# The down product of a feed-forward group, cut into pieces that run between the next group's gate and up products

## The chip, the cores and the metric

The kernel runs on one core of one Trainium2 chip. The metric is the device time of one execution in microseconds (us). Engines are named as in the profile: PE (matrix products; PEld is its weight load), DVE (vector engine), ACT (scalar engine, which reads PSUM and applies functions), POOL (GpSimd), SP (which issues most DMAs). PE's results lie in PSUM tiles, from which DVE and ACT read them; the kernel counts PSUM in banks of 128 x 512 fp32 values and hands out eight in the part that changes.

## What is computed

Two model blocks one after the other on 512 tokens of width 1024 (528 tokens in the second one, with 16 meta tokens ahead). The second block has two layers, and each ends in the feed-forward part that the change touches:

```python
def conv_ffn(h, w_up, w_gate, conv_w, conv_b, w_down):
    u = h @ w_up
    g = h @ w_gate
    g = lax.conv_general_dilated(g, conv_w[:, None, :], window_strides=(1,),
                                 padding=[(CONV_WIDTH - 1, 0)], ...) + conv_b
    return (jax.nn.silu(g) * u) @ w_down

h = h + conv_ffn(rmsnorm(h, norm_ffn[l]), ...)       # l = 0, 1
return rmsnorm(h, norm_final)[:, N_META:N_META + S]
```

The inner width is 2816 = 22 feature blocks of 128. Everything is fp32; the kernel splits each operand into a rounded high part and a low remainder and adds three products (high x high, low x high, high x low) for each matrix product.

## The kernel before, in words

Activations stand transposed: features on the 128 partitions, tokens along the row. `X` (eight blocks of 128 features) is the residual stream. `ffn(l, out)` (L1052) runs the feed-forward part twice: for l = 0 with 528 columns, for l = 1 with 512 and with the final norm at its end.

- `seven` (L1109) prepares the normed input as the right operands of seven half-size products.
- `paired` (L1158) makes one gate or up product for the two feature blocks i and i + 11 at once. It loads two weight tiles, adds and splits them (DVE at L1170 and L157, ACT at L156), and then runs seven products of 12 matmuls each. In the program's order these are 1, 5, 6, 2, 7, 4, 3. Products 1, 6, 7, 4 add up in one bank (`pa`, tag "a", two buffers), 5 and 3 in `pc`, 2 in `pb` (one tile of two banks, tag "mm"). After product 7 ACT copies `pa` to `f` (L1204), and product 4 must wait for that copy, because it adds to `pa`. DVE adds `pc` to `f` (L1205) before product 3. Afterwards L1208 adds both banks to the result `e`, and L1095 or L1100 read `pa`.
- One round i of the loop (L1086) is a gate `paired`, the convolution, silu (ACT, L1074) and a multiplication on POOL (L1075), an up `paired`, and the products of both, split into `aH`, `aL` (`done`, L1078).
- Rounds stand in groups (0,3), (3,6), (6,9), (9,11) (L1083). After a group, `added` (L685) multiplies its 6 (or 4) feature blocks with the down weights: for each of eight output blocks o one weight tile (`weights`, L138: DMA on SP's queue, ACT rounds, DVE subtracts) and 36 matmuls (18 of double width for 512 columns), and then DVE adds the PSUM tile to `X` (L695). I call these eight products a burst. The last group of l = 1 goes through `final` (L1211), which also makes the final norm; its eight products per half of the columns take PSUM tiles of tags "mm" and "a" in turn.
- `Banks` (L36) hands out PSUM: tag "mm" turns over the mm pools, here two of two banks each; "t" and "a" have two single banks each.

The order of instructions on each engine is set by a scheduler from the program's order, dependencies and buffers; each engine then runs its list strictly in that order, and waits for others by semaphores. The code that makes it:

Of the kernel before, what the change touches and what calls it, by code (L numbers as in the profile page):

```python
# [9 lines left out]
F32 = mybir.dt.float32  # L10
F32R = mybir.dt.float32r
AF = mybir.ActivationFunctionType
OP = mybir.AluOpType
# [5 lines left out]
S = 512  # L19
# [11 lines left out]
def two(x):  # L31

    return x.rearrange("p (a b) -> p a b", a=2)


class Banks:  # L36
# [7 lines left out]
    def tile(self, *args, tag, bufs, **opts):  # L44
        if tag == "mm":
            tag, bufs, self.n = f"mm{self.n % self.mm}", 1, self.n + 1
        return self.pools[tag].tile(*args, tag=tag, bufs=bufs, **opts)


class Norm:  # L50
# [42 lines left out]
class Net:  # L93
# [617 lines left out]
    W = 1360  # L711
# [340 lines left out]
    def ffn(self, l, out=None):  # L1052

        nc, d = self.nc, self.d
        X, n, u = (self.X, T2, 0) if l == 0 else (self.X[:, :, TAIL:], S, NM - TAIL)
        lead, w = u or 2, n + u
        m = w // 2
        self.tb, self.mm = 2, 2
        with ExitStack() as c:
            pp = Banks(self.tc, c, "ffn", "mm1 t a mm0")  # L1060
            fp = c.enter_context(self.tc.tile_pool(name="ffn", bufs=1))
            new = lambda name, cols, bufs, dt=F32: fp.tile([128, cols], dt, name=name, tag=name, bufs=bufs)
            cw = fp.tile([128, 22, 4], F32, name="cw")
            nc.gpsimd.dma_start(cw, d[f"conv_{l}"])
            ops, rs = self.seven(pp, fp, X, self.gain[:, 6 + l])
            act = [], []

            def activated(i, g):

                z = new("z", n, 4)  # L1070
                nc.scalar.activation(z, g[:, lead:], AF.Identity, scale=cw[:, i, 2:3], bias=cw[:, i, 3:4])  # L1071
                for k in range(2):
                    nc.vector.scalar_tensor_tensor(z, g[:, lead - 2 + k:lead - 2 + k + n], cw[:, i, k:k + 1], z, op0=OP.mult, op1=OP.add)  # L1073
                nc.scalar.activation(z, z, AF.Silu)  # L1074
                nc.gpsimd.tensor_tensor(z, z, rs[:, u:], op=OP.mult)  # L1075
                return z

            def done(z):  # L1078
                act[0].append(new("aH", n, 7, F32R))
                act[1].append(new("aL", n, 7, F32R))  # L1080
                self.split(act[0][-1], act[1][-1], z)

            for a, b in ((0, 3), (3, 6), (6, 9), (9, 11)):  # L1083
                act[0].clear()
                act[1].clear()
                for i in range(a, b):  # L1086
                    g = [new("g", lead + n, 3) for _ in range(2)]
                    if u == 0:
                        for t in g:
                            nc.vector.memset(t[:, :2], 0.0)  # L1090
                    e = g[0][:, lead - u:]
                    f, t = self.paired(pp, fp, d[f"gate_{l}"], i, ops, e, m)
                    nc.vector.tensor_tensor(e, e, rs, op=OP.mult)
                    nc.vector.scalar_tensor_tensor(g[1][:, lead - u + m:], f, -1.0, rs[:, m:], op0=OP.mult, op1=OP.mult)
                    nc.vector.scalar_tensor_tensor(g[1][:, lead - u:lead - u + m], t, -1.0, rs[:, :m], op0=OP.mult, op1=OP.mult)  # L1095
                    z = [activated(i + 11 * j, g[j]) for j in range(2)]
                    e = new("u", w, 2)
                    f, t = self.paired(pp, fp, d[f"up_{l}"], i, ops, e, m)
                    nc.vector.scalar_tensor_tensor(z[1][:, m - u:], f, -1.0, z[1][:, m - u:], op0=OP.mult, op1=OP.mult)
                    nc.vector.scalar_tensor_tensor(z[1][:, :m - u], t[:, u:], -1.0, z[1][:, :m - u], op0=OP.mult, op1=OP.mult)  # L1100
                    nc.vector.tensor_tensor(z[0], z[0], e[:, u:], op=OP.mult)
                    for t in z:
                        done(t)
                if out is None or b < 11:
                    self.added(pp, d[f"down_{l}"], act, 2 * a, 2 * b, X[:, :, u:])
                else:
                    self.final(pp, fp, d[f"down_{l}"], act, 2 * a, 2 * b, out)

    def seven(self, pp, fp, x, g):  # L1109

# [44 lines left out]
            nc.scalar.activation(rs[:, a:b], out, AF.Copy)  # L1155
        return right, rs

    def paired(self, pp, fp, src, i, right, e, m):  # L1158


        nc, wp = self.nc, self.wp
# [21 lines left out]
        h, l = half(new("wy", 1))  # L1183
# [6 lines left out]
        def product(ps, j, start=False):  # L1190
            (wh, wl), (bh, bl) = left[j], right[j]
            for k in range(4):
                for v, (p, q) in enumerate(((wh, bh), (wh, bl), (wl, bh))):
                    nc.tensor.matmul(ps, p[:, k], q[k], start=start and k == 0 and v == 0, stop=k == 3 and v == 2, skip_group_check=not start)  # L1194

        f = fp.tile([128, T2 // 2], F32, name="f", tag="f", bufs=2)[:, :m]
# [6 lines left out]
        product(pa, 7)  # L1203
        nc.scalar.activation(f, pa, AF.Copy)  # L1204
        nc.vector.tensor_tensor(f, f, pc, op=OP.add)  # L1205
        product(pa, 4)
        product(pc, 3)
        nc.vector.tensor_tensor(two(e), two(e), pt[:, :, :m], op=OP.add)  # L1208
        return f, pa

    def final(self, pp, fp, src, act, a, b, out):  # L1211


        nc, x, m = self.nc, self.X[:, :, NM:], S // 2
        W = [[(0, b - a, self.weights(src[o, :, a:b], o >= 4))] for o in range(8)]
        rows = [fp.tile([128, T2], F32, name="o", tag="op", bufs=12) for _ in range(8)]
        for i in range(2):
            c = slice(m * i, m * i + m)
            sums, y = self.sums(pp, m, 8, 1), [t[:, c] for t in rows]
            for o in range(8):  # L1220
                _, _, ps = self.bank(pp, 0, m, ("mm", "a")[o % 2], 2)
                for k, e, w in W[o]:
                    self.dense([([(ps, c)], w)], (act[0][k:e], act[1][k:e]), k == 0, e == b - a)
                nc.vector.tensor_tensor(x[:, o, c], x[:, o, c], ps, op=OP.add)
                sums(x[:, o, c])
                nc.scalar.activation(y[o], x[:, o, c], AF.Copy, scale=self.gain[:, 8, o:o + 1])
            rs = self.row_tile("rs", m)
            (ps, _, _), = self.rstd(pp, sums, 1.0 / D)
            nc.scalar.activation(rs, ps, AF.Copy)
            for k in range(8):  # L1230
                if k in (5, 7):
                    nc.gpsimd.tensor_tensor(y[k], y[k], rs, op=OP.mult)
                else:
                    nc.vector.tensor_tensor(y[k], y[k], ps, op=OP.mult)  # L1234
                (nc.sync if k % 2 else nc.scalar).dma_start(out[:, k, c], y[k])
# [118 lines left out]
```

## Time and profile before

| what | value |
|---|---|
| three runs | 2217.07, 2216.91, 2213.74 us; median 2216.91 us |
| profiled execution | 2216.71 us, of which the span of its instructions is 2215.0 us |
| PE busy | 2052.8 us, 93% of the span |
| DVE busy | 1488.5 us, 67% |
| ACT busy | 986.6 us, 45% |
| granted PE clock over the span | 0.98 of full speed |

Busy time is the time in which an instruction of the engine runs. For PE it hides something: a matmul is recorded longer than the distance to the next one, so a short pause between two matmuls is partly covered by the record of the first. The rows further down are windows (busy time by engine in a stretch), waits (for whom an engine stood idle), timelines and groups of instructions. Times in windows and timelines count from the start of the span.

### The profile page before, as it was taken

Reading aid. Unit: us, or ns where it says so; the run is one execution under the profiler, and the core shown is the slowest. Engines: PE = TensorE matmul, PEld = TensorE weight load, DVE = VectorE, ACT = ScalarE, POOL = GpSimd, SP = SyncE. Lnnn points to the kernel's source line nnn. Section 1 sums busy time; section 2 is a strip of 40 time slices with the busy share of each in tenths; the row PEclk is TensorE's granted clock in tenths of the full one; section 3 lists DMA queues with packets and bytes.
Section 4 is the critical chain, followed back from the end, with each engine's and each line's share of the span. In section 5 each row is a group of like instructions: output and inputs, shape, how many; then the busy total and the mean of one; then the engine's idle time right before and its main releaser. Section 6 shows DMA issues by size and latency. Waiting matters only on the chain. (4 is left out here: it accounts for less than half of the span.)

```text
span 2215.0 us, 36664 instructions
## 1 busy us (share of the span) xinstructions
PE 2052.8 (93%) x14384; PEld 1865.7 (84%) x14384; DVE 1488.5 (67%) x2490; ACT 986.6 (45%) x1799; POOL 554.2 (25%) x652
## 2 busy tenths in 40 slices
PE   8999999999989999999889898999999988989897
PEld 6788888788889899989779797988888977878787
DVE  5566766666577994564876767675555787676775
ACT  5454644455555222453543434344333454343434
POOL 2222232222145553650010101013354201010101
PEclk9999999999999999999999999999999989999999
DMA  6643125533224222532122222224423312222222
GB/s 191 178 113 98 56 91 159 159 92 87 74 69 129 81 86 77 156 107 78 67 91 81 91 82 91 77 91 116 117 79 97 97 67 91 81 91 81 91 81 67
DMA packets 77324, 216.54 MB, mean 98 GB/s; under 512 B 11128, under 2 KB 14736, under 8 KB 77152
## 3 DMA queue, kind: packets, MB, share of 16 engines
q1 hardware_dynamic: 73520, 205.93, 31.3%
q0 software_dynamic: 2336, 7.19, 1.1%
q8 instruction: 113, 1.85, 0.3%
q10 hardware_dynamic: 1296, 1.09, 0.2%
q14 instruction: 59, 0.48, 0.1%
HBM read 166.20 MB, written 6.92 MB: 78 GB/s over the span
## 5 line engine op out<-in xcount | busy, mean ns | idle before, releaser
L166 PE MATMUL ps_mm<-hH,wh 128*128 128x264 f32 (+3 forms) x1480 | 393.5, 323 | 18.7 <-DVE t L190 7.6
L166 PE MATMUL ps_mm<-hL,wh 128*128 128x264 f32 (+3 forms) x1480 | 396.0, 321 | 10.8 <-DVE hL L70 10.8
L166 PE MATMUL ps_mm<-hH,wl 128*128 128x264 f32 (+3 forms) x1480 | 394.6, 320 | 0.0
L150 ACT ACTIVATE wh<-wr 128x1024 fp32r<-128x1024 f32 (+3 forms) x229 | 212.0, 929 | 321.3 <-PE ps_mm L166 243.0
L151 DVE TENSOR_TENSOR wl<-wr,wh 128x1024 fp32r<-128x1024 f32 (+3 forms) x205 | 229.2, 1121 | 85.0 <-ACT wh L150 81.2
L166 PEld LDWEIGHTS ps_mm<-hH,wh 128*128 128x128 f32 (+1 forms) x1480 | 250.2, 192 | 39.5 <-DVE t L190 7.8
L166 PEld LDWEIGHTS ps_mm<-hL,wh 128*128 128x128 f32 (+1 forms) x1480 | 251.6, 192 | 28.9 <-DVE hL L70 12.5
L166 PEld LDWEIGHTS ps_mm<-hH,wl 128*128 128x128 f32 (+1 forms) x1480 | 251.8, 192 | 17.9 <-issue 1.4
L1075 POOL TENSOR_TENSOR z<-z,rs 128x528 f32<-128x528 f32 (+1 forms) x44 | 68.6, 1574 | 689.8 <-ACT z L1074 689.8
L166 PE MATMUL ps_mm<-aH,wh 128*128 128x264 f32 (+2 forms) x528 | 137.6, 318 | 10.6 <-DVE u L1208 5.7
L166 PE MATMUL ps_mm<-aL,wh 128*128 128x264 f32 (+2 forms) x528 | 137.4, 315 | 0.0
L166 PE MATMUL ps_mm<-aH,wl 128*128 128x264 f32 (+2 forms) x528 | 136.7, 313 | 0.0
L1194 PE MATMUL ps_a<-h,wh 128*128 128x264 f32 (+1 forms) x528 | 105.6, 293 | 27.1 <-DVE z L1100 23.5
L190 DVE TENSOR_TENSOR t<-ps_mm,rs 128x528 f32<-128x528 f32 (+1 forms) x101 | 70.2, 695 | 86.3 <-PE ps_mm L166 81.0
L695 DVE TENSOR_TENSOR X<-X,ps_mm 128x528 f32<-128x528 f32 (+2 forms) x88 | 60.5, 694 | 98.5 <-PE ps_mm L166 98.3
L1194 PEld LDWEIGHTS ps_a<-h,wh 128*128 128x128 f32 x528 | 84.7, 194 | 32.6 <-issue 13.6
L166 PEld LDWEIGHTS ps_mm<-aH,wh 128*128 128x128 f32 x528 | 86.8, 188 | 20.8 <-DVE u L1208 7.2
L166 PE MATMUL ps_mm<-yH,wh 128*128 128x264 f32 (+2 forms) x392 | 95.3, 308 | 0.2 <-DVE X L695 0.2
L166 PE MATMUL ps_mm<-yH,wl 128*128 128x264 f32 (+2 forms) x392 | 94.9, 308 | 0.0
L166 PE MATMUL ps_mm<-yL,wh 128*128 128x264 f32 (+2 forms) x392 | 93.7, 305 | 0.0
L166 PEld LDWEIGHTS ps_mm<-aL,wh 128*128 128x128 f32 x528 | 87.7, 188 | 6.5 <-DVE aL L157 0.4
L166 PEld LDWEIGHTS ps_mm<-aH,wl 128*128 128x128 f32 x528 | 87.5, 188 | 6.5
(335 smaller groups left out, 4954.6 us busy)
## 6 DMA issues: line engine op xcount, KB each, us to landing
wr<-w1c SPq DMA_DIRECT2D x52, 512.0 KB, 3.9
wr<-gate SPq DMA_DIRECT2D x44, 512.0 KB, 3.3
wr<-up SPq DMA_DIRECT2D x44, 512.0 KB, 3.2
wr<-down SPq DMA_DIRECT2D x48, 384.0 KB, 3.1
ks<-st SPq DMA_DIRECT2D x48, 264.0 KB, 5.2
wr<-we_b SPq DMA_DIRECT2D x24, 512.0 KB, 3.5
wr<-wo_c SPq DMA_DIRECT2D x24, 512.0 KB, 3.4
qs<-st SPq DMA_DIRECT2D x64, 132.0 KB, 3.0
```

The source lines that it names most:

```text
L150: nc.scalar.activation(high, raw, AF.Copy)
L151: getattr(nc, eng).tensor_tensor(low, raw, high.bitcast(F32), op=OP.subtract)
L166: self.nc.tensor.matmul(p[:a.shape[2]], a[:, k], b[k][:, t], start=bool(first and k == 0 and j == 0), stop=bool(last and k == len(ah) - 1 ...
L190: self.nc.vector.tensor_tensor(f(out), v, f(r), op=OP.mult)
L695: self.nc.vector.tensor_tensor(f(x[:, o]), f(x[:, o]), v, op=OP.add)
L1075: nc.gpsimd.tensor_tensor(z, z, rs[:, u:], op=OP.mult)
L1194: nc.tensor.matmul(ps, p[:, k], q[k], start=start and k == 0 and v == 0, stop=k == 3 and v == 2, skip_group_check=not start)
```

## The change

The bursts are gone. There are six groups of rounds, (0,1), (1,3), (3,5), (5,7), (7,9), (9,11). After a group its activations are kept, and its down product becomes eight units, one for each output block: for two-round groups 24 matmuls (12 of double width for 512 columns), for the first group half of that. `paired` calls `between` twice, ahead of product 4 and ahead of product 3, and a call runs units of the group before. For a two-round group that makes one unit at each of its eight places. The units of the last group run after the last round as before (l = 0), or in `final` (l = 1). One weight tile of 1024 columns serves two units (four for the first group).

PSUM: tag "t" has no pool of its own in this part any more. A third pair of banks, mm2, takes its place, so paired tiles and units share three bank pairs in turn, and the sums of the norms lie in such a pair (`Turns`). In `final` all products take tag "a" alone, two single banks.

```diff
--- before.py
+++ after.py
@@ -45,6 +45,19 @@
         if tag == "mm":
             tag, bufs, self.n = f"mm{self.n % self.mm}", 1, self.n + 1
         return self.pools[tag].tile(*args, tag=tag, bufs=bufs, **opts)
+
+
+class Turns(Banks):
+
+
+    def tile(self, *args, tag, bufs, name=None, **opts):
+        if tag != "t":
+            return super().tile(*args, tag=tag, bufs=bufs, name=name, **opts)
+        if name == "ps_ss":
+            self.norm = super().tile([128, 2, 512], F32, tag="mm", bufs=1, name="ps_n")
+            self.parts = [self.norm[:, 1, :256], self.norm[:, 0]]
+            return self.norm[:, 1, 256:]
+        return self.parts.pop()
 
 
 class Norm:
@@ -1057,13 +1070,13 @@
         m = w // 2
         self.tb, self.mm = 2, 2
         with ExitStack() as c:
-            pp = Banks(self.tc, c, "ffn", "mm1 t a mm0")
+            pp = Turns(self.tc, c, "ffn", "mm1 mm2 a mm0")
             fp = c.enter_context(self.tc.tile_pool(name="ffn", bufs=1))
             new = lambda name, cols, bufs, dt=F32: fp.tile([128, cols], dt, name=name, tag=name, bufs=bufs)
             cw = fp.tile([128, 22, 4], F32, name="cw")
             nc.gpsimd.dma_start(cw, d[f"conv_{l}"])
             ops, rs = self.seven(pp, fp, X, self.gain[:, 6 + l])
-            act = [], []
+            act, units = ([], []), []
 
             def activated(i, g):
 
@@ -1080,31 +1093,64 @@
                 act[1].append(new("aL", n, 7, F32R))
                 self.split(act[0][-1], act[1][-1], z)
 
-            for a, b in ((0, 3), (3, 6), (6, 9), (9, 11)):
+            def after(a, b):
+
+                high, low = list(act[0]), list(act[1])
                 act[0].clear()
                 act[1].clear()
+                kc = 2 * (b - a)
+                W = {}
+
+                def unit(o):
+                    t = 8 // kc
+                    if o % t == 0:
+                        v = self.weights(d[f"down_{l}"][o:o + t, :, 2 * a:2 * b].rearrange("o p k n -> p o (k n)"))
+                        for j in range(t):
+                            W[o + j] = [x[:, j].rearrange("p (k n) -> p k n", n=128) for x in v]
+                    _, ps, v = self.bank(pp, 0, n)
+                    self.dense([(ps, W[o])], (high, low))
+                    f = two if n > S else lambda x: x
+                    nc.vector.tensor_tensor(f(X[:, o, u:]), f(X[:, o, u:]), v, op=OP.add)
+
+                return [lambda o=o: unit(o) for o in range(8)]
+
+            slots = 0
+
+            def between():
+
+                nonlocal slots
+                for _ in range(-(-len(units) // max(slots, 1))):
+                    units.pop(0)()
+                slots -= 1
+
+            cuts = (0, 1, 3, 5, 7, 9, 11)
+            for a, b in zip(cuts, cuts[1:]):
+                slots = 4 * (b - a)
                 for i in range(a, b):
                     g = [new("g", lead + n, 3) for _ in range(2)]
                     if u == 0:
                         for t in g:
                             nc.vector.memset(t[:, :2], 0.0)
                     e = g[0][:, lead - u:]
-                    f, t = self.paired(pp, fp, d[f"gate_{l}"], i, ops, e, m)
+                    f, t = self.paired(pp, fp, d[f"gate_{l}"], i, ops, e, m, between)
                     nc.vector.tensor_tensor(e, e, rs, op=OP.mult)
                     nc.vector.scalar_tensor_tensor(g[1][:, lead - u + m:], f, -1.0, rs[:, m:], op0=OP.mult, op1=OP.mult)
                     nc.vector.scalar_tensor_tensor(g[1][:, lead - u:lead - u + m], t, -1.0, rs[:, :m], op0=OP.mult, op1=OP.mult)
                     z = [activated(i + 11 * j, g[j]) for j in range(2)]
                     e = new("u", w, 2)
-                    f, t = self.paired(pp, fp, d[f"up_{l}"], i, ops, e, m)
+                    f, t = self.paired(pp, fp, d[f"up_{l}"], i, ops, e, m, between)
                     nc.vector.scalar_tensor_tensor(z[1][:, m - u:], f, -1.0, z[1][:, m - u:], op0=OP.mult, op1=OP.mult)
                     nc.vector.scalar_tensor_tensor(z[1][:, :m - u], t[:, u:], -1.0, z[1][:, :m - u], op0=OP.mult, op1=OP.mult)
                     nc.vector.tensor_tensor(z[0], z[0], e[:, u:], op=OP.mult)
                     for t in z:
                         done(t)
                 if out is None or b < 11:
-                    self.added(pp, d[f"down_{l}"], act, 2 * a, 2 * b, X[:, :, u:])
-                else:
-                    self.final(pp, fp, d[f"down_{l}"], act, 2 * a, 2 * b, out)
+                    units += after(a, b)
+            if out is None:
+                for unit in units:
+                    unit()
+            else:
+                self.final(pp, fp, d[f"down_{l}"], act, 2 * a, 2 * b, out)
 
     def seven(self, pp, fp, x, g):
 
@@ -1155,7 +1201,7 @@
             nc.scalar.activation(rs[:, a:b], out, AF.Copy)
         return right, rs
 
-    def paired(self, pp, fp, src, i, right, e, m):
+    def paired(self, pp, fp, src, i, right, e, m, between):
 
 
         nc, wp = self.nc, self.wp
@@ -1203,7 +1249,9 @@
         product(pa, 7)
         nc.scalar.activation(f, pa, AF.Copy)
         nc.vector.tensor_tensor(f, f, pc, op=OP.add)
+        between()
         product(pa, 4)
+        between()
         product(pc, 3)
         nc.vector.tensor_tensor(two(e), two(e), pt[:, :, :m], op=OP.add)
         return f, pa
@@ -1218,7 +1266,7 @@
             c = slice(m * i, m * i + m)
             sums, y = self.sums(pp, m, 8, 1), [t[:, c] for t in rows]
             for o in range(8):
-                _, _, ps = self.bank(pp, 0, m, ("mm", "a")[o % 2], 2)
+                _, _, ps = self.bank(pp, 0, m, "a", 2)
                 for k, e, w in W[o]:
                     self.dense([([(ps, c)], w)], (act[0][k:e], act[1][k:e]), k == 0, e == b - a)
                 nc.vector.tensor_tensor(x[:, o, c], x[:, o, c], ps, op=OP.add)
```

How the scheduler lays this out is seen at three places. The first is PE in the gate product of round 4 (l = 0), from the last matmul of product 7 (written to `ps_a_12917`) to the first ones of product 4 (those with `wy`); `ps_a_13050` is the next paired product. Before:

```order
L1194 MATMUL ps_a_12917<-op_11448,wl_12907 128x264
L1194 MATMUL ps_a_13050<-h_11350,wx_13043 128x264
L1194 MATMUL ps_a_13050<-h_11349,wx_13043 128x264
L1194 MATMUL ps_a_12917<-h_11348,wy_12914 128x264
L1194 MATMUL ps_a_12917<-h_11347,wy_12914 128x264
```

With the change the gate's bank is called `ps_a_12803`, the next one `ps_a_12994`; `ps_mm_13067` and `ps_mm_13105` are units:

```order
L1240 MATMUL ps_a_12803<-op_11448,wl_12793 128x264
L1240 MATMUL ps_a_12994<-h_11350,wx_12987 128x264
L1240 MATMUL ps_a_12994<-h_11349,wx_12987 128x264
L179 MATMUL ps_mm_13067<-aH_12058,wh_13062 128x264 x2
L179 MATMUL ps_mm_13067<-aL_12059,wh_13062 128x264 x2
L179 MATMUL ps_mm_13105<-aH_12058,wh_13062 128x264 x2
L179 MATMUL ps_mm_13105<-aL_12059,wh_13062 128x264 x2
L1240 MATMUL ps_a_12803<-h_11348,wy_12800 128x264
```

Eight matmuls of two units have moved in ahead of product 4, beside the two of the next paired product that stood there already. At the other three paired products of two rounds (l = 0) 24 or more unit matmuls stand there.

The second place is DVE in the same gate product, from the addition to `f` on. Before:

```order
L1205 TENSOR_TENSOR f_12919<-f_12919,ps_mm_12918 128x264
L1094 SCALAR_TENSOR_TENSOR g_12889<-f_12919,rs_11463 128x264
L1095 SCALAR_TENSOR_TENSOR g_12889<-ps_a_12917,rs_11463 128x264
L157 TENSOR_TENSOR wy_13047<-wr_13026,wy_13047 128x512
L157 TENSOR_TENSOR wx_13044<-ws_13030,wx_13043 128x1024
L1208 TENSOR_TENSOR g_12888<-g_12888,ps_mm_12918 128x528
L1170 TENSOR_TENSOR ws_13162<-wr_13157,ws_13161 128x512
L1093 TENSOR_TENSOR g_12888<-g_12888,rs_11463 128x528
```

With the change (`ps_mm_13067` and `ps_mm_13105` are the two units, `wl_13170` is a weight split that stood elsewhere):

```order
L1251 TENSOR_TENSOR f_12805<-f_12805,ps_mm_12804 128x264
L170 TENSOR_TENSOR wl_13170<-wr_13159,wh_13169 128x1024
L1137 SCALAR_TENSOR_TENSOR g_12775<-f_12805,rs_11463 128x264
L1138 SCALAR_TENSOR_TENSOR g_12775<-ps_a_12803,rs_11463 128x264
L170 TENSOR_TENSOR wy_12991<-wr_12970,wy_12991 128x512
L170 TENSOR_TENSOR wx_12988<-ws_12974,wx_12987 128x1024
L1256 TENSOR_TENSOR g_12774<-g_12774,ps_mm_12804 128x528
L1113 TENSOR_TENSOR X_66<-X_66,ps_mm_13067 128x528
L1216 TENSOR_TENSOR ws_13164<-wr_13159,ws_13163 128x512
L1136 TENSOR_TENSOR g_12774<-g_12774,rs_11463 128x528
L1113 TENSOR_TENSOR X_66<-X_66,ps_mm_13105 128x528
```

Two additions to `X`, each of which waits for the last matmul of its unit, have moved in among the steps of the gate product and of the next weights.

The third place is PE at the end of l = 1, where the first activations of the last round (`aH_22735` before, `aH_22699` with the change) come into the last down product. Before, four tiles are open:

```order
L166 MATMUL ps_mm_22835<-aH_22476,wl_22757 128x256
L166 MATMUL ps_mm_22800<-aH_22735,wh_22744 128x256
L166 MATMUL ps_mm_22817<-aH_22735,wh_22750 128x256
L166 MATMUL ps_mm_22835<-aH_22735,wh_22756 128x256
L166 MATMUL ps_mm_22853<-aH_22735,wh_22762 128x256
```

With the change two are:

```order
L179 MATMUL ps_mm_22781<-aH_22372,wl_22715 128x256
L179 MATMUL ps_mm_22764<-aH_22699,wh_22708 128x256
L179 MATMUL ps_mm_22781<-aH_22699,wh_22714 128x256
L179 MATMUL ps_mm_22764<-aL_22700,wh_22708 128x256
L179 MATMUL ps_mm_22764<-aH_22699,wl_22709 128x256
```

Of the matmuls that need only earlier activations, 24 stood ahead of this place before, and 12 do now; the other tiles must wait until one of two banks is free.

On SP's queue the eight down loads of a group (384 KB each, in runs of 3 KB) become four of 512 KB in runs of 2 KB (two for the first group, runs of 1 KB), each between a paired product's two loads and the next ones. Outside the feed-forward parts the engines' lists stand as they were, but for a few rows at the seams.

## Rows read from the trace of the kernel before

**Rows 1.** The page: the span, and PE's busy us, share and records.

```profile
span 2215.0 us, 36664 instructions
...
PE 2052.8 (93%) x14384; PEld 1865.7 (84%) x14384; DVE 1488.5 (67%) x2490; ACT 986.6 (45%) x1799; POOL 554.2 (25%) x652
```

**Rows 2.** Windows: us; PE, PEld, DVE, ACT, POOL busy; clock; DMA.

```profile
1165.20:1276.20 111.00, 100.18 (x794) 97.20 (x793) 79.46 (x119) 46.20 (x69) 10.18 (x6) 1.00 0.26 86
1193.00:1276.30 83.30, 72.79 (x571) 70.03 (x570) 61.48 (x97) 37.55 (x60) 10.18 (x6) 1.00 0.23 74
1166.00:1193.00 27.00, 27.00 (x222) 27.00 (x223) 17.28 (x22) 7.96 (x9) 0.00 (x0) 1.00 0.38 125
1885.20:1994.00 108.80, 97.92 (x649) 88.40 (x648) 79.68 (x113) 45.84 (x69) 9.50 (x6) 1.00 0.27 88
1912.00:1994.00 82.00, 71.44 (x534) 67.24 (x533) 62.20 (x91) 37.70 (x60) 9.50 (x6) 1.00 0.23 75
```

**Rows 3.** Waits of PE (us, times, longest), l = 0, rounds 0 to 10.

```profile
PE ps_a L1194 <- ACT f L1204: 16.9, 18, 1.1
PE ps_a L1194 <- DVE z L1100: 11.1, 7, 2.4
PE ps_a L1194 <- DVE wx L157: 4.8, 4, 1.2
PE ps_mm L166 <- DVE u L1208: 2.5, 3, 0.8
PE ps_mm L1194 <- DVE f L1205: 1.1, 1, 1.1
PE ps_mm L166 <- DVE X L695: 0.9, 3, 0.3
```

**Rows 4.** The same for l = 1.

```profile
PE ps_a L1194 <- ACT f L1204: 18.0, 18, 1.7
PE ps_a L1194 <- DVE z L1100: 12.4, 7, 2.4
PE ps_a L1194 <- DVE wx L157: 4.1, 4, 1.2
PE ps_mm L166 <- DVE u L1208: 2.4, 3, 0.8
```

**Rows 5.** Timeline of PE (start, length, engine, line, operation) at one wait.

```profile
1129.30 0.41 PE L1194 MATMUL ps_a<-h,wx 128*128 128x264 f32 x2
1130.56 0.63 PE L1194 MATMUL ps_a<-h,wy 128*128 128x264 f32 x3 [0.85 <-ACT f L1204]
```

**Rows 6.** Timeline of PE inside a burst of down products.

```profile
1160.13 0.40 PE L166 MATMUL ps_mm<-aH,wl 128*128 128x264 f32 x2
...
1162.31 0.40 PE L166 MATMUL ps_mm<-aH,wl 128*128 128x264 f32 x2
```

**Rows 7.** DVE groups (xcount | busy us, mean ns), 1193 to 1304 us.

```profile
L151 DVE TENSOR_TENSOR wl<-wr,wh 128x768 fp32r<-128x768 f32 x8 | 7.6, 964 | 3.0 <-ACT wh L150 3.0
L157 DVE TENSOR_TENSOR wl<-wr,wh 128x1024 fp32r<-128x1024 f32 x6 | 7.3, 1223 | 2.9 <-ACT wh L156 2.8
...
L695 DVE TENSOR_TENSOR X<-X,ps_mm 128x528 f32<-128x528 f32 x9 | 6.2, 703 | 13.4 <-PE ps_mm L166 13.4
```

**Rows 8.** Timeline of PE where the last down product begins.

```profile
2179.86 0.39 PE L166 MATMUL ps_mm<-aH,wh 128*128 128x256 f32 x1 [1.57 <-DVE z L1100]
...
2182.32 0.73 PE L166 MATMUL ps_mm<-aH,wh 128*128 128x256 f32 x4 [0.82 <-ACT aH L156]
```

**Rows 9.** A window at the head of the first feed-forward block.

```profile
1040.00:1100.00 60.00, 52.77 (x379) 50.03 (x379) 51.19 (x88) 32.29 (x54) 1.97 (x2) 0.91 0.26 85
```

**Rows 10.** DMA issues in 1166 to 1193 us: KB each, median us to landing.

```profile
wr<-gate SPq DMA_DIRECT2D x3, 512.0 KB, 3.3
...
wr<-down SPq DMA_DIRECT2D x2, 384.0 KB, 3.9
```


## The prediction

> **What bounds the kernel now.** First the page, then windows over the feed-forward parts, then who waits for whom there. The page gives PE 2052.8 us of a span of 2215.0 [rows 1]: PE is the engine to look at, and a change pays by what it takes from PE's pauses. The windows show where they are. One period of l = 0 runs from the first addition to X of one burst to that of the next: three rounds and one burst, 111.0 us, with PE busy for 100.18 and DVE for 79.46 [rows 2]. Inside it, 27.0 us of burst have PE busy for all 27.00, and the 83.3 us of rounds only for 72.79. So the rounds wait and the burst does not. In l = 1 it is the same: 108.8 us, PE 97.92. The granted clock is 1.00 in all these rows, the higher of the two levels (2.4 GHz), so the clock is no part of it.
>
> Waits next. From round 0's up product to the last rounds, PE of l = 0 waits 36 times: for ACT's copy `f` (16.9 us), for DVE's reading of the older `pa` bank (`z` L1100, 11.1), for a weight split (`wx`, 4.8), for the last round's result before a burst (`u`, 2.5), and 2.0 for the rest; together 37.3 us [rows 3]. For l = 1 it is 35 times and 37.8 us [rows 4]; its 0.9 us for additions to X read as in rows 3. Per period that is 10 waits. All are of one kind: a chain over ACT, POOL or DVE that PE has nothing to put beside, while burst matmuls that need none of it stand in the list later.
>
> **What a wait costs.** More than its row says. At 1129 us two matmuls stand in a row of 0.41 us, of which the second takes 0.28, so it started at 1129.43; the next started at 1130.56 [rows 5]. Undisturbed matmuls follow each other in 0.121 us (18 from 1160.13 to 1162.31, nine rows of two) [rows 6]. The wait cost 1.13 - 0.12 = 1.01 us where the row says 0.85: 0.16 more. I add 0.16 to each: 75.1 + 71 x 0.16 = 86.5 us for both layers.
>
> The period confirms this. By PE's busy time its pauses are 111.0 - 100.18 = 10.8 us, by PEld's 111.0 - 97.20 = 13.8 us [rows 2]; ten waits with 0.16 each give about 12.2. The Trainium skill ("Perfetto Trace Analysis", section "Identifying the Most-Contended Engine") says that matmul busy time is no good measure of the headroom, since pipelined matmuls look different in the trace, and that weight-load busy time is one. By the rule the period could give 13.8 us and by matmul records 10.8; scaled to the 86.5 us that would be 98 and 77 us. The trace agrees with the rule more than with matmul busy time; the sum goes by the waits.
>
> **The change part by part.**
>
> *PE's work* is the same: the same matmuls of the same widths. What changes is what stands beside the waits.
>
> *Cover for `f`.* Between product 7 and product 4 two matmuls stood and now at least ten; at three of four paired products of two rounds it is 26 or more. To cover 0.85 to 1.1 us of wait with its 0.16 and the two matmuls already there takes 1.25 to 1.5 us. Ten matmuls are 1.21, 26 are 3.1. So three in four waits go and the fourth leaves up to 0.25 us: 10 places x 0.25 = 2.5 us stay.
>
> *Cover for `z` and `wx`.* A paired product of 84 matmuls gets up to 48 more beside it, 5.8 us, and POOL's and DVE's chains (longest wait 2.4 us [rows 3]) have that time in addition. These go, and so do the `u` waits before bursts. What is late next on PE is `f`, which then has the shortest cover.
>
> *What stays.* Round 0 has no unit to put in. Its up product keeps one `f` wait (1.1) and one `z` wait (2.4), with 0.32 for the two restarts 3.8; ten matmuls of the next round now stand before the latter, which takes off 1.2. Twice 2.6 is 5.2 us.
>
> *More for DVE.* Three rounds now bring twelve additions to X and not eight: 4 x 0.703 = 2.8 us; and six splits of 1024 columns instead of eight of 768: 6 x 1.223 - 8 x 0.964 = -0.4 us [rows 7]. DVE then has 79.46 + 2.4 = 81.9 us in the 111.0 - 12.2 = 98.8 us that PE needs, 83%; in l = 1 79.68 + 2.4 = 82.1 in 96.6, 85%. It has been at 51.19 of 60 us, 85%, at the head of l = 0 [rows 9]. So there is room, but little, and I cost DVE's work itself at nothing because PE's matmuls hide it; without that cover it is the first rival.
>
> *New waits.* Each addition to X stands on DVE until its unit is done, with weight splits and the gate's steps behind it, and PE waits for these. And three bank pairs serve a paired product and two units, so that a paired product comes back to the bank pair of the one before and needs DVE's last addition there. No row of before shows either. Below, the cost is nothing: in the lists whole products lie between. Above, one split of DVE in the way of every paired product: 1.22 + 0.16, over the 40 of rounds 1 to 10 in both layers 55 us. The nearest row is PE waiting for an addition to X: 0.9 us in three waits [rows 3], 0.3 + 0.16 = 0.46. I take that at every second paired product: 20 x 0.46 = 9.2 us.
>
> *SP's queue and the DMAs.* Down tiles of 512 KB come one per paired product between its own loads. In the burst window, with the DMA share at 0.38 [rows 2], gate loads of 512 KB landed after 3.3 us and down loads after 3.9 [rows 10], and PE waited for none. A paired product with two units will take some 16 us. I cost this at nothing, hidden by the tiles being loaded one paired product ahead; without that cover it is the second rival.
>
> *The end of l = 1.* Twelve and not 24 matmuls stand ready when the last round's activations come. PE already waits there: 1.57 us before the open tiles and 0.82 in them [rows 8]. The six that are missing after the last up product are 6 x 0.12 = 0.7 us of cover less, and the third tile must wait until DVE has read the first, which is about as much: 1.5 us lost.
>
> **Sum.** 86.5 - 2.5 - 5.2 - 9.2 - 1.5 = 68.1 us gained. The profiled execution took 2216.71 us, 1.7 beyond its span and 0.2 from the median of the runs, so one number serves for both: 2216.7 - 68.1 = 2148.6, about 2149 us. The likeliest case's own range: no new waits and full cover give 2137; new waits of 0.46 at twice as many paired products and a little more give 2160 to 2175. Below 2132 little is to be had, since 86.5 us are all the waits there are.
>
> **Rivals.**
>
> *DVE becomes the bound.* In the rounds of before DVE is busy for 61.48 of 83.3 us, 74%, and in l = 1 for 62.20 of 82.0, 76% [rows 2]. If its in-order list can't go above that when additions to X stand waiting in it, three rounds take 81.9 / 0.74 = 110.7 us against 111.0 and 82.1 / 0.76 = 108.0 against 108.8: nothing is gained (2213 us). At 79 and 80% it is 103.7 and 102.6; with 3.3 periods in each layer 45 us are gained, 2172. For it speaks that the waiting additions are new in the rounds; against it that in the rounds before it was PE's waiting that held DVE up, and the 85% [rows 9]. The Trainium skill ("PSUM — Partial Sum Buffer", section "Engine vs sequencer instructions") says that DVE's queue is strictly first in, first out. By it a waiting addition holds up all that is behind it, which speaks against this change; the order rows show what that is, but no row shows its price. Chance of 2175 to 2213: 14%.
>
> *Weights come late: slower.* Two raw buffers now serve a gate or up tile and a down tile in each paired product, and three of four rounded tiles are taken per paired product, not two. If a load can only start when the tile before is split, a landing (3.3) and a split (1.22), 4.5 us, get near PE's path. Half of it exposed at each of 40 paired products, with 0.16, costs 40 x 2.4 = 96 us in place of my 9.2: 2236 us. It decides from (68.1 + 9.2) / 40 = 1.9 us per paired product. Against it: a paired product takes three times as long as that chain, and the burst row. 8%.
>
> *The units cover the wrong place.* The change does not do what it says if `f` stays late, because ACT has the units' weight tiles before it or product 4 gets its units too early. Then 16.9 + 18.0 + 36 x 0.16 = 40.7 us stay and not 2.5: 2187 us. Against it are the ten or more matmuls in the list. 8%.
>
> **How the numbers follow.** The forecast, 2132 to 2175, has 66%; below it 4%; the rivals 14, 8 and 8. The range of 8 in 10 is 2132 to 2190: it leaves out the low end (4), the upper half of the DVE case (7), and the slower one (8). A measurement of this kernel tells 0.2%, some 4 us, from no change. Faster: 66 + 4 + 8 + 10 of the DVE case, 88%; the rest of the DVE case, 4%, is no change; slower 8%.
>
> **What would show it.** Waits of PE for `f` should fall from 16.9 us to under 5 in each layer, and those for `z` to one wait of round 0. Three rounds should take about 100 us in l = 0, with PE's weight loads busy for 95% or more and DVE for 80% or more. The time outside the two feed-forward parts should be the same within 3 us. It is wrong if PE's waits for DVE's splits, additions to X or ACT's rounding grow to 20 us a layer, or if DVE has no idle time and PE waits.

## The result, and the profile after

The changed kernel took 2142.27 us (median of four runs, 2138.65 to 2149.06), the kernel before 2215.68 (2213.74 to 2217.07): a ratio of 0.9673, 95% interval 0.9645 to 0.9701. That is 73 us less, where 68 were forecast (2149 us). The profiled execution took 2140.01 us, 76.7 less than that of before [rows 1]:

```profile
span 2138.3 us, 36583 instructions
...
PE 2034.8 (95%) x14384; PEld 1863.6 (87%) x14384; DVE 1518.1 (71%) x2506; ACT 980.4 (46%) x1783; POOL 570.6 (27%) x652
```

By the first and last matmul of each part, l = 0 went from 429.0 to 388.2 us (40.8 less) and l = 1 with the end of the program from 435.9 to 403.2 (32.7 less). Between the layers it is 290.4 and 291.1. The remaining 3.8 us lie ahead of l = 0, where the lists are the same; over the profiles of the runs below, which differ nowhere in that part, l = 0 starts anywhere from 1053 to 1063 us, so they are not the change's.

Windows, as in rows 2: two rounds of l = 0 with their units, four such periods, and most of l = 1.

```profile
1230.80:1295.00 64.20, 64.20 (x528) 64.20 (x528) 55.79 (x81) 30.35 (x44) 8.42 (x4) 1.00 0.31 99
1165.40:1420.00 254.60, 254.57 (x2088) 254.60 (x2089) 218.29 (x308) 118.65 (x173) 32.46 (x16) 1.00 0.30 97
1850.00:2090.00 240.00, 236.52 (x1607) 218.28 (x1607) 205.37 (x284) 109.85 (x163) 24.76 (x14) 1.00 0.29 92
```

For 254.60 us PE has 0.03 us of pause and its weight loads none. 528 matmuls in 64.20 us are 0.1216 us each, the undisturbed distance [rows 6]. Three rounds take 1.5 x 64.2 = 96.3 us where they took 111.0 [rows 2], 14.7 less. PE's pauses by matmul records had been 10.8, by waits with their restarts 12.2, by weight loads 13.8. The Trainium skill's rule that the prediction weighed ("Perfetto Trace Analysis", section "Identifying the Most-Contended Engine": weight-load busy time, not matmul busy time, tells the headroom) is what these rows of l = 0 bear out; the sum by waits was too small here. In l = 1 the trace does not agree with it: weight loads left 108.8 - 88.40 = 20.4 us of a period free [rows 2], but three rounds of the change take 96.5 us (four take 128.7, from 1908.1 to 2036.8), only 12.3 less. A double-width matmul takes 0.234 us there and its weight load 0.19, so loads are not busy all the time even where PE never waits.

PE's waits (us, times, longest) over all of l = 0, 1040 to 1475 us, against rows 3:

```profile
PE ps_a L1240 <- DVE wx L170: 1.7, 1, 1.7
...
PE ps_mm L179 <- DVE u L1256: 1.6, 1, 1.6
...
PE ps_a L1240 <- DVE z L1143: 1.3, 2, 0.8
PE ps_a L1240 <- ACT f L1250: 1.2, 2, 0.7
```

The wait for `f` fell from 16.9 us to 1.2, the one for `z` from 11.1 to 1.3. What is left stands for the most part in round 0, at the first units behind it and at the last ones. In l = 1 (1750 us to the end), against rows 4:

```profile
PE ps_mm L179 <- ACT aH L169: 4.1, 1, 4.1
PE ps_a L1240 <- DVE z L1143: 3.3, 3, 1.1
PE ps_a L1240 <- ACT f L1250: 3.2, 4, 1.3
...
PE ps_a L1240 <- DVE wx L170: 1.2, 1, 1.2
```

`f` went from 18.0 to 3.2 and `z` from 12.4 to 3.3. The first row is new. It is the place of rows 8, and the ACT timeline shows what holds it up, the PE timeline how long, the windows the granted clock:

```profile
2096.81 1.27 ACT L163 ACTIVATE wH<-wr 128x512 fp32r<-128x512 f32 x2 [2.87 <-DMA wr<-down]
2100.77 0.63 ACT L163 ACTIVATE wH<-wr 128x512 fp32r<-128x512 f32 x1 [2.69 <-DMA wr<-down]
2101.31 1.13 ACT L169 ACTIVATE aH<-z 128x512 fp32r<-128x512 f32 x2
```

```profile
2101.97 0.80 PE L179 MATMUL ps_mm<-aH,wh 128*128 128x256 f32 x2 [4.12 <-ACT aH L169]
```

```profile
2097.00:2102.00 5.00, 0.88 (x9) 0.68 (x7) 3.06 (x5) 2.30 (x5) 0.00 (x0) 0.95 0.36 105
2102.00:2106.00 4.00, 3.90 (x15) 3.31 (x16) 2.77 (x6) 1.61 (x4) 0.00 (x0) 0.50 0.00 0
2106.00:2110.00 4.00, 4.00 (x27) 4.00 (x27) 1.46 (x4) 1.69 (x5) 0.00 (x0) 0.71 0.00 0
```

ACT's list has the rounding of a down tile ahead of the split of the last activations. The tile lands late, ACT stands 2.69 us, and PE has six matmuls left to run and then nothing for 4.12 us. After that the clock is at its lower level (0.50 of full speed, 1.2 GHz) and 42 matmuls take 8 us, which at 0.12 are 5: up to 3 us more (two short waits are in the 8 us).

Last, DVE's additions to X in 1165 to 1420 us (xcount | busy us, mean ns | idle before), against the last of rows 7:

```profile
L1113 DVE TENSOR_TENSOR X<-X,ps_mm 128x528 f32<-128x528 f32 x32 | 22.0, 697 | 0.3
```

Before, DVE stood 13.4 us in front of nine of them. Now it stands 0.3 us in front of 32: when DVE comes to an addition, its unit is done.

### The profile page after: what moved, and what is told of

Read it like the earlier page. It is cut to its first block, busy times and chain, and to the rows that moved or that the text cites. A ratio compares the mean times of both kernels' runs of the same rounds, so it can differ in the third digit from the quotient of the medians.

```text
span 2138.3 us, 36583 instructions
## 1 busy us (share of the span) xinstructions
PE 2034.8 (95%) x14384; PEld 1863.6 (87%) x14384; DVE 1518.1 (71%) x2506; ACT 980.4 (46%) x1783; POOL 570.6 (27%) x652
## 5 line engine op out<-in xcount | busy, mean ns | idle before, releaser
L1088 POOL TENSOR_TENSOR z<-z,rs 128x528 f32<-128x528 f32 (+1 forms) x44 | 82.9, 1900 | 591.4 <-ACT z L1087 591.4
L169 ACT ACTIVATE wh<-ws 128x1024 fp32r<-128x1024 f32 x44 | 46.6, 1059 | 126.3 <-PE ps_mm L179 80.0
```

The lines of the kernel that those rows point to most:

```text
L169: self.nc.scalar.activation(high, x, AF.Copy)
```

## The experiments

Ratios are to the kernel before on the same chip, with 95% intervals. The theory throughout is the prediction's: PE waits for chains over ACT and DVE, and matmuls that need none of it, put in front, take the waits away.

**Six groups, but bursts.** All of the change except the place of the units: they run right after their own group.

```diff
-                    units += after(a, b)
+                    for unit in after(a, b):
+                        unit()
```

> The units of a group run as a burst right after it, as before the change; six groups, three bank pairs, the new weight tiles and the tail stay. Theory (the gain is PE's waits covered by units): the waits for f, z, wx and u come back, more than 50 us in both layers, and the time is 2200 to 2225 us. Rival (the gain comes from smaller groups, bank pairs or weight tiles, whatever stands beside the waits): 2165 us or less.

2269.43 us, 1.0228 (1.0192 to 1.0264): slower than before by some 50 us. The place of the units is the whole of the gain and more. That the finer groups by themselves cost so much had not been expected; the run with three bank pairs alone, below, tells part of why.

**Two bank pairs.** The change without `Turns`.

```diff
-            pp = Turns(self.tc, c, "ffn", "mm1 mm2 a mm0")
+            pp = Banks(self.tc, c, "ffn", "mm1 t a mm0")
```

> The units stay between the products, but with two bank pairs and two single banks for the sums, as before the change. Theory (cover is what pays, banks only let it happen): most of the gain stays, 2145 to 2170 us, with small waits of PE for DVE's additions (e L1256, X L1113) at the bank pairs. Rival (three bank pairs in turn are what frees PE): 2190 us or more.

2131.16 us, 0.9606 (0.9577 to 0.9635): faster than the change, and outside what either theory gave. In l = 0 the two are alike (first paired matmul to the norm behind: 394.8 us, the change 395.3); from l = 1 on to the end it is 392.5 against 403.2. The window of l = 1, its only wait, and two windows of the end:

```profile
1850.00:2090.00 240.00, 238.70 (x1635) 220.56 (x1633) 212.31 (x283) 109.50 (x165) 30.70 (x16) 1.00 0.29 93
```

```profile
PE ps_mm L1240 <- DVE f L1251: 1.3, 7, 0.2
```

```profile
2097.00:2102.00 5.00, 4.65 (x39) 4.66 (x40) 3.43 (x8) 3.76 (x10) 0.00 (x0) 1.00 0.18 52
2102.00:2106.00 4.00, 4.00 (x36) 4.00 (x35) 2.29 (x7) 2.56 (x8) 0.00 (x0) 1.00 0.00 0
```

The three waits for `z` are gone, and so is the long one at the end, with the clock's fall. The order of PE differs there: of the last units, twelve matmuls of double width now stand behind the last paired product and not ahead of it:

```profile
2089.17 0.89 PE L1240 MATMUL ps_mm<-op,wx 128*128 128x258 f32 x6
2090.87 0.39 PE L179 MATMUL ps_mm<-aH,wh 128*128 128x256 f32 x1 [0.82 <-DVE z L1143]
...
2091.67 0.39 PE L179 MATMUL ps_mm<-aH,wh 128*128 128x512 f32 x1
```

**Groups of one round.** From the second round on a group is one round (the last stays at two).

```diff
-            cuts = (0, 1, 3, 5, 7, 9, 11)
+            cuts = (0, 1, 2, 3, 4, 5, 6, 7, 8, 9, 11)
```

> Groups of one round (the last one stays (9,11)): units of half the matmuls, twice as many additions to X, so DVE would have about 60.8 of 64.2 us per two rounds where it has 55.8 now. Theory (PE is the bound and DVE has room left): 2140 to 2155 us. Rival (DVE is at its limit at 86% busy): two rounds take 60.8 / 0.86 = 70.7 us, about 60 us more in all, 2200 us.

2139.9 us, 0.9642 (0.9612 to 0.9672), as the change. The window and the waits of l = 0, 1165 to 1420 us:

```profile
1165.00:1420.00 255.00, 250.37 (x2034) 248.25 (x2033) 228.94 (x337) 112.74 (x169) 30.51 (x16) 1.00 0.28 94
```

```profile
PE ps_a L1240 <- DVE wx L170: 3.9, 8, 1.2
```

Twice the additions to X bring DVE to 228.94 of 255 us, 90%, and only now does PE wait in these rounds for a split that comes late, 3.9 us.

**More work for DVE.** Each unit adds once more, into a tile that nobody reads: 88 additions in all.

```diff
                     nc.vector.tensor_tensor(f(X[:, o, u:]), f(X[:, o, u:]), v, op=OP.add)
+                    extra = new("u", w, 2)[:, :n]
+                    nc.vector.tensor_tensor(f(extra), f(X[:, o, u:]), v, op=OP.add)
```

> The changed kernel with one more DVE addition of the same size after each addition to X (it reads the same two operands and its result goes unused): 88 of them, 0.62 us apart, 55 us of DVE work and nothing else. Theory (DVE has room): less than 20 us more, 2142 to 2162 us. Rival (DVE at its limit): all of it is paid, 2195 us.

2167.51 us, 0.9767 (0.9738 to 0.9795): 25 us over the change (21 by the ratios), for 1572.6 - 1518.1 = 54.5 us more of DVE. Windows and waits (1165 to 1425 us, and 1850 to 2100 us):

```profile
1165.00:1425.00 260.00, 253.97 (x2049) 250.46 (x2049) 234.35 (x339) 118.53 (x172) 29.77 (x16) 1.00 0.29 95
1850.00:2100.00 250.00, 235.69 (x1572) 212.15 (x1571) 224.82 (x307) 111.70 (x162) 31.66 (x16) 1.00 0.29 93
```

```profile
PE ps_a L1242 <- DVE g L1140: 3.7, 4, 0.9
```

```profile
PE ps_a L1242 <- DVE wx L170: 5.4, 6, 0.9
PE ps_a L1242 <- DVE g L1140: 4.2, 4, 1.1
```

Both theories are half right. DVE reaches 90% in both layers and PE waits for it while DVE still has a tenth of the window free: its list is in order, and the steps that PE needs stand behind additions that it doesn't need. Ahead of PE's wait of 0.92 us at 1189.83, DVE runs two additions to X (1.31 us from 1186.55 on) and a split before it reads the bank that PE waits for. But this run does not load DVE alone. The tile that nobody reads is one of the two buffers of `u`, so ACT's copies to `u` wait for the added work (ACT's waits, 1165 to 1425 us):

```profile
ACT u L1246 <- DVE u L1115: 8.7, 4, 2.2
```

The 25 us are the price of both; the runs don't tell them apart. So the rival of DVE as the bound was not absurd, its signs show at 90% here; the change stands at 55.79 of 64.20, 87%. The share alone does not settle it: with two bank pairs DVE is busy for 212.31 of 240 us, 88%, and PE waits for 1.3 us.

**A dose.** Four groups as before, and the units only in the first round of the next group: three of eleven rounds are covered.

```diff
-            cuts = (0, 1, 3, 5, 7, 9, 11)
+            cuts = (0, 3, 6, 9, 11)
...
-                slots = 4 * (b - a)
+                slots = 4
```

> A dose test. The four groups of the kernel before are kept, and a group's eight units run only in the first round of the next group, four paired products with two units each, so that three of the eleven rounds of a layer are covered and eight are as before. Theory of the prediction (each round's waits go where other matmuls stand in front of them, about 6 to 7 us a round): 2 layers x 3 rounds x 6.5 us = some 39 us, less round 0 of l = 0 that is never covered; 2175 to 2192 us. Rival (the gain came from the three bank pairs or from the finer groups, which hold in every round): with three bank pairs in all rounds the gain would be most of the 73 us, under 2160. Rival (units anywhere only move waits): no gain, over 2210.

2170.93 us, 0.9803 (0.9780 to 0.9826), a little under the theory's lower end. Windows of 30 us inside a covered round and its waits with those of the two uncovered rounds behind it (1161 to 1267 us):

```profile
1163.00:1193.00 30.00, 30.00 (x249) 30.00 (x248) 22.06 (x32) 12.81 (x18) 3.01 (x2) 1.00 0.33 105
```

```profile
PE ps_a L1240 <- ACT f L1250: 2.0, 2, 1.1
PE ps_a L1240 <- ACT u L1247: 1.5, 1, 1.5
PE ps_a L1240 <- DVE wx L170: 1.2, 1, 1.2
```

Every one of these waits that took over 0.3 us began after 1227 us, in the uncovered rounds. So the waits are tied to the cover, round by round. Ahead of the window, where the covered stretch begins, two still stand: 2.05 us for `f` at 1151 and 1.20 for `wx` at 1157.

The total proves less than it seems. This run has the three bank pairs in every round, and the next run shows that these alone, with the same groups, come to 2188.77 us, 0.9860. Against that, the six covered rounds of both layers gain 13 us by the ratios and 18 by the medians, 2 to 3 us a round and not the 6.5 of the expectation. Most of the 46 us below the kernel before is the bank pairs', so that the time fell near the expected range by luck.

**Three bank pairs alone.** The run of the bursts with four groups, which leaves of the change only `Turns` (with tag "a" in `final`, and the wider down tiles for the last group of l = 0).

```diff
-            cuts = (0, 1, 3, 5, 7, 9, 11)
+            cuts = (0, 3, 6, 9, 11)
```

> One part alone: the kernel before with its four groups and its bursts of eight units, but with three bank pairs in turn. Theory (the waits are for results on their way through ACT and DVE, not for a free bank; the pairs free nothing without cover): within 15 us of the kernel before, 2202 to 2232. With it the burst kernel with six groups (2269) pays some 50 us for four bursts more, that is for the ends of groups. Rival (the pairs cost by themselves, since the bursts use banks that the paired products then want): 2240 to 2270, and the six groups cost little. Rival (the pairs are what frees PE): under 2190.

2188.77 us, 0.9860 (0.9830 to 0.9890): 31 us faster than before, which the theory had excluded; it lies just inside the range of the rival that the pairs free PE. In the traces the two feed-forward parts are 19 us shorter (428.6 to 417.7 us for l = 0, from its first gate matmul to its last down matmul, 435.9 to 427.5 for l = 1 with the end). Two periods, and the waits of l = 0 (1040 to 1480 us), against rows 2 and rows 3:

```profile
1158.60:1265.70 107.10, 99.42 (x792) 97.22 (x792) 81.37 (x118) 46.04 (x68) 9.18 (x6) 1.00 0.28 89
1265.70:1372.60 106.90, 99.33 (x792) 97.12 (x792) 80.36 (x119) 46.00 (x68) 9.81 (x6) 1.00 0.27 89
```

```profile
PE ps_a L1241 <- ACT f L1251: 9.9, 11, 1.3
PE ps_a L1241 <- ACT u L1248: 6.6, 7, 1.4
PE ps_a L1241 <- DVE wx L170: 5.0, 4, 1.4
...
PE ps_a L1241 <- DVE z L1143: 1.0, 1, 1.0
```

The `z` waits go (11.1 to 1.0 us), those for `f` fall to 9.9, and waits for ACT's copy `u` come in (6.6). Part of what the prediction took for late results was a list that too few banks had forced. With a third pair, 24 matmuls of the next paired product (`ps_mm`, those with `wh` and `wl`) run ahead of the wait for `z` in round 1, which is down to 0.96 us from 2.36; before, they stand behind it. That is cover too, of another kind:

```profile
1107.04 0.29 PE L1241 MATMUL ps_mm<-h,wl 128*128 128x264 f32 x1
...
1112.32 0.52 PE L1241 MATMUL ps_a<-h,wh 128*128 128x264 f32 x2 [0.96 <-DVE z L1143]
```

The Trainium skill says so of consistent bubbles: they can mean that there is too little PSUM for the next tile ("Perfetto Trace Analysis", section "Optimization Strategy"). This run agrees, by 31 us (19 in the traces); the run with two bank pairs shows that cover removes the same bubbles without any more banks. The two gains don't add up.

It also tells where the first run lost its time. Two of its periods, of two rounds each, with the waits of the second (1257.3 to 1335.4 us):

```profile
1178.70:1257.40 78.70, 68.45 (x529) 66.27 (x529) 56.71 (x81) 30.67 (x44) 7.07 (x4) 0.98 0.26 83
1257.40:1335.50 78.10, 68.29 (x529) 66.10 (x529) 56.66 (x81) 30.45 (x44) 7.01 (x4) 0.98 0.25 83
```

```profile
PE ps_mm L179 <- DVE u L1257: 2.5, 1, 2.5
```

A round costs 39.2 us there and 35.7 with four groups; 3.5 x 22 rounds = 77 us of the 81 by which these two runs differ. Shorter groups mean more ends, and at each end a burst waits for results of the round just before it (2.5 us here, at most 0.8 in rows 3). And the clock falls there. Windows of 4 us, the last two ahead of one end and the one after another:

```profile
1178.00:1182.00 4.00, 3.12 (x13) 2.82 (x13) 3.29 (x8) 0.81 (x2) 0.00 (x0) 0.59 0.34 122
...
1250.00:1254.00 4.00, 2.41 (x19) 2.19 (x20) 4.00 (x8) 2.53 (x4) 2.30 (x2) 1.00 0.09 23
1254.00:1258.00 4.00, 1.51 (x11) 1.29 (x10) 3.66 (x6) 0.00 (x0) 1.64 (x1) 0.90 0.77 236
```

PE runs 19 and then 11 matmuls in 4 us, where an undisturbed window has 33, and the granted clock falls to 0.90 and behind the end to 0.59. 41% of 4 us are 1.6 us; if all ten ends are like this one, 16 us of the 81; the waits for `u` are 13 us more over the whole trace (19.6 for 6.4); in the periods of four groups the clock is 1.00. What makes up the rest of the 81 us is open.

**The end of l = 1.** The change, with `final` on two tags again, and every second of its weight tiles in a spare buffer, so that its load can start early.

```diff
+        spare = lambda o: fp.tile([128, 1024], F32, name="ws", tag="ws", bufs=2) if o % 2 else None
-        W = [[(0, b - a, self.weights(src[o, :, a:b], o >= 4))] for o in range(8)]
+        W = [[(0, b - a, self.weights(src[o, :, a:b], o >= 4, raw=spare(o)))] for o in range(8)]
...
-                _, _, ps = self.bank(pp, 0, m, "a", 2)
+                _, _, ps = self.bank(pp, 0, m, ("mm", "a")[o % 2], 2)
```

> The changed kernel, but the last down products take their banks from two tags in turn, as before the change, and every second of their weight tiles lands in a spare buffer, so that it needs no free raw buffer and its transfer starts early. Theory (the 4.1 us for which PE stands at the end of l = 1 come from down weights that land late: ACT waits for them and holds the split of the last activations behind them, and the clock that fell to 0.50 after it costs some 3 us more): the wait goes, the clock stays at 1.00, 4 to 7 us below the changed kernel: 2135 to 2138 us, a ratio of 0.9635 to 0.965. Rival (the activations would be late without that, as the chain from the last up product to the last split is the same): the wait stays at 3 us or more, and the time within 2 us of 2142.

2141.74 us, 0.9670 (0.9647 to 0.9692): nothing gained. PE's waits at the end (2095 to 2136 us) and the clock:

```profile
PE ps_n L256 <- DVE accd L249: 1.9, 1, 1.9
PE ps_mm L179 <- DVE wl L164: 1.5, 1, 1.5
PE ps_mm L179 <- DVE o L1283: 1.2, 1, 1.2
...
PE ps_mm L179 <- ACT aH L169: 0.4, 1, 0.4
```

```profile
2100.00:2105.00 5.00, 4.51 (x35) 4.31 (x36) 3.56 (x8) 0.29 (x1) 0.00 (x0) 1.00 0.00 0
2105.00:2110.00 5.00, 4.59 (x37) 4.31 (x37) 2.58 (x6) 1.51 (x4) 0.00 (x0) 1.00 0.00 0
```

The wait fell to 0.4 us and the clock stayed at 1.00, as the theory said, but 4.6 us came back as three waits for DVE in the same stretch, and from the start of l = 1 to the end the profile is only 2.2 us shorter (401.0 for 403.2). The cause of the wait was right, what its end is worth was wrong: with these banks the end is a chain over DVE and ACT, with little for PE to do beside it.

**Versions of two bank pairs.** First with `final` on two tags, then with the spare buffers as well; edits as above.

> The kernel with two bank pairs in turn (the one of the first experiments that ran 10 us faster than the change), with the last down products on two tags in turn. It starts as that one, whose two waits for a sum of X in the last stretch took 1.1 us together: those go if the banks were what they waited for. Theory: 0.5 to 1.5 us less, ratio 0.959 to 0.961. Rival (PE has no use for an earlier bank, because the sums stand in DVE's order): no change, 0.9600 to 0.9612.

> The same, and every second weight tile of the last down products in a spare buffer. Theory (with two bank pairs the tail has more cover, and late weights cost 0.8 to 1.8 us there at most): 1 to 3 us less than with two bank pairs alone, ratio 0.9585 to 0.9600. Rival: the transfers were not late for PE, within 1 us of it. It is the candidate for the fastest version.

2128.54 us, 0.9602 (0.9580 to 0.9624), and 2126.25 us, 0.9595 (0.9572 to 0.9618). Neither can be told from two bank pairs alone. In the first the two waits for X are gone, but one of 1.4 us for `accd` is in their place. The second was run again, with the change beside it:

> The changed kernel once more, beside the next one on the same chip, so that the two can be set against each other: 2138 to 2148 us, a ratio of 0.965 to 0.969.

> The fastest version so far once more: units of the change, two bank pairs in turn, two tags and spare buffers in the last down products. If it beats the change, 2122 to 2131 us here, and 10 us or more under the run of the change on the same chip; if its lead was the chip's, less than 5 us under it.

The change 2143.94 us (2137.25 to 2148.24), 0.9664 (0.9641 to 0.9688); the candidate 2128.27 us (2123.13 to 2130.47), 0.9591 (0.9568 to 0.9614). The ranges don't meet: it beats the change by some 15 us. The change's wait at the end was there again, 4.2 us.

## Why the prediction was right, and where it was not

The mechanism was right: the same matmuls, and cover where PE stood. Without the new place of the units the rest of the change is a loss (2269 us), with the units and the bank pairs of before the gain is 88 us, and in covered rounds the waits are gone but for a few. That the sum came to 68 us where 73 were measured is in part luck, since errors of both signs stand in it. By its steps:

- *The waits*: 86.5 us in all was too little. Three rounds of l = 0 gave 14.7 us where waits with restarts promised 12.2, and with two bank pairs cover gained 88 us although round 0's waits stayed, more than the 86.5 that the prediction took for all the waits there are. The 98 us that it scales from the weight loads of l = 0 is nearer.

- *Cover for `f`*: 2.5 us were to stay besides round 0's; 1.2 and 3.2 us did, in all of l = 0 and l = 1 with round 0.
- *Cover for `z` and `wx`*: held in l = 0. In l = 1 three `z` waits of 1.1 us stayed. They go with two bank pairs; why the third pair brings them there is open. Around the first of them (1905 to 1909 us) DVE is busy for all 4.00 us, with weight splits ahead of the reading that PE waits for.
- *Round 0*: 5.2 us were to stay in both layers. The wait for `z` behind it (2.4 us) fell to 0.5 in l = 0, but one for a split (`wx`, 1.7) and small ones came: seven of 5.4 us together (1085 to 1112 us), and eight of 5.6 in l = 1 (1764 to 1794). With 0.16 for each that is some 13 us, 8 more than forecast; nothing was gained there.
- *DVE*: 83 and 85% forecast, 87% (55.79 of 64.20) and 86% (205.37 of 240) measured. Enough room, but 90%, where PE waited for it in two runs, is near.
- *New waits*: 9.2 us forecast, none stood in the 255 us of l = 0. This term was mis-sized by all of it. The nearest row was of a burst, where DVE stood waiting for PE; in the rounds it is behind PE, and finds its units done (0.3 us idle before 32 additions).
- *SP's queue and the DMAs*: nothing in the rounds, as costed. The Trainium skill's rule of strictly first in, first out queues ("PSUM — Partial Sum Buffer", section "Engine vs sequencer instructions") was feared for DVE; the trace showed its price on ACT, at the end, where a late down tile held up the last activations.
- *The end of l = 1*: 1.5 us forecast. The wait is 4.1 us and the lower clock costs up to 3 more, where rows 8 have 1.57 + 0.82. From the last paired matmul to the end it is 41.4 us where it was 37.0, with six matmuls (0.7 us) more in it: 3.7 us lost. The prediction costed cover and two banks, and had no term for a late transfer on ACT's list. Taking that away returned 2 us at most.
- *The bank pairs* were costed only as a source of new waits. Alone they gain 31 us, with cover they cost 11 to 15 (2142 against 2131, and the repeats). The prediction gave cover the credit for waits that either removes; that did no harm to the sum, because cover removes nearly all of them.

As an estimate from these figures: 68.1, and 11.5 for the waits (98 for 86.5), and 9.2 for new waits that didn't come, less 8 for round 0, 3.8 for the `z` waits of l = 1 (3.3 + 3 x 0.16) and 2.2 for the end, makes some 75 us, where 73 were measured.

Rivals: *DVE becomes the bound* is what the run with more work for DVE begins to show, at 25 us for 54.5, ACT's waits for the buffer included. *Weights come late* shows at the end. *Wrong place* fell with the `f` waits.

## What to carry to other kernels

Where an engine waits for chains over others in every round, matmuls that are ready anyway and stand later in a block are worth more between those waits than any shortening of the chains; size the gain by the pauses in the weight loads where these fill a stretch without waits (l = 0 here), and not where the matmuls are so wide that they don't (l = 1). Ask of each remaining wait whether it is for a result or for a bank, because cover and more banks remove the same ones and don't add. And finer pieces pay only if they are moved: left in place, each group's end is one more wait.

## What the runs showed of the hardware

- After 5 us with nine matmuls in them (a wait of 4.12 us) the granted clock stood at 0.50 and 0.71 for 8 us; in the run with spare buffers a wait of 1.5 us in the same stretch left it at 1.00. It also fell, to 0.59, where no wait was over 2.5 us but only 30 matmuls ran in 8 us (the ends of the bursts with six groups).
- PE ran 2088 matmuls of 264 columns without a pause of its weight loads in 254.60 us, 0.122 us each, while DVE was at 86% and the DMAs at 0.30.
- DVE work added to a list that was 87% full cost about half of its time, 21 to 25 of 54.5 us (ACT's waits for the shared buffer included), with a tenth of the engine's time still free.
- A matmul of 512 columns with a weight load of its own took 0.234 us (nine from 2084.62 to 2086.73 us in the change), one of 264 columns 0.122.
